# Cross-entropy on one core: rows p and 128+p on partition p, loads divided at the row end, results transposed on VectorE and stored in 128-byte pieces

## The chip, the core and the metric

One core of a Trainium2 chip. The metric is the device time of one execution in microseconds (us), as a median over runs. ScalarE is ACT, VectorE DVE, GpSimd POOL and SyncE SP in the profile; "SPq" is SP's sequencer, which issues the loads of logits and the stores here.

## The reference

For 256 rows of 32,000 float32 logits and one label per row, the kernel returns `log(sum(exp(x))) - x[label]`:

```python
def reference(logits, labels):
    log_probs = logits - np.max(logits, axis=-1, keepdims=True)
    log_probs = log_probs - np.log(np.sum(np.exp(log_probs), axis=-1, keepdims=True))
    return np.array([-log_probs[i, labels[i]] for i in range(batch)]).astype(np.float32)
```

The 32.77 MB of logits have to be read once; 1 KB goes out.

## The kernel before

Partition p holds rows 2p and 2p+1 one after the other, 64,000 columns, which arrive in 14 loads of falling size. ScalarE takes exp of each chunk with a running sum. The logit of the label is gathered, `eg = exp(-g)`, and the result is `Ln(sum * eg)`.

```python
CHUNKS = [14848, 12288, 8832, 6528, 4992, 3776, 2752,
          2368, 1856, 1344, 1344, 1152, 1024, 896]
flat = logits.rearrange("(p r) c -> p (r c)", r=ROWS)
# ... tiles; load(i) issues one chunk, exps(i) sums its exp (two sums where a chunk crosses the row end)
with tc.manual_schedule():
    for i in range(HEAD):
        load(i)
    # ... labels (one 16-byte piece per partition), idx, two indirect gathers into g
    exps(0)
    # ... exps(1), the later loads
    nc.scalar.activation(out=eg[:, :], in_=g[:, :], func=AF.Exp, scale=-1.0)
    # ... exps(2) to exps(12); Ln of the first row on the way
    nc.vector.reduce_sum(out=sums[:, 1:2], in_=parts[1][:, :], axis=mybir.AxisListType.X)
    nc.vector.tensor_mul(out=bias[:, :], in0=sums[:, 1:2], in1=eg[:, 1:2])
    exps(len(CHUNKS) - 1)
    nc.scalar.activation(
        out=res[:, 1:2], in_=s_last[:, :], func=AF.Ln, scale=eg[:, 1:2], bias=bias[:, :]
    )
    nc.sync.dma_start(out=out.rearrange("(p r) -> p r", r=ROWS), in_=res[:, :])
```

The last line stores 128 pieces of 8 bytes, one from each partition, which fill 1 KB of HBM.

The softmax here doesn't subtract the row's maximum and nothing guards it: scores larger than these inputs give would overflow.

Of the kernel before, what the change touches and what calls it, by code (L numbers as in the profile page):

```python
# [2 lines left out]

# [4 lines left out]

P = 128
ROWS = 2  # L10
F32 = mybir.dt.float32
I32 = mybir.dt.int32
AF = mybir.ActivationFunctionType

CHUNKS = [
    14848, 12288, 8832, 6528, 4992, 3776, 2752,
    2368, 1856, 1344, 1344, 1152, 1024, 896,
]
HEAD = 5


@with_exitstack
def kernel(
    ctx: ExitStack,
    tc: tile.TileContext,
    logits: bass.AP,
    labels: bass.AP,
    out: bass.AP,
):
    nc = tc.nc  # L30
    B, C = logits.shape
    assert B == P * ROWS and sum(CHUNKS) == ROWS * C


    flat = logits.rearrange("(p r) c -> p (r c)", r=ROWS)


    pieces = []
    starts = []
    at = 0  # L40
    for n in CHUNKS:
        starts.append(at)
        cuts = [at] + [c for c in range(C, ROWS * C, C) if at < c < at + n] + [at + n]
        pieces.append([(a, b, a // C) for a, b in zip(cuts, cuts[1:])])
        at += n

    head = ctx.enter_context(tc.tile_pool(name="head", bufs=1))
    small = ctx.enter_context(tc.tile_pool(name="small", bufs=1))

    tiles = []  # L50
    for i in range(HEAD):
        tiles.append((head.tile([P, CHUNKS[i]], F32, name=f"x{i}", tag=f"slot{i}"), starts[i]))
    mid = head.tile([P, CHUNKS[1]], F32, name="x_mid", tag="slot1")
    tail = head.tile([P, CHUNKS[0]], F32, name="x_tail", tag="slot0")
    tiles.append((mid, starts[HEAD]))
    for i in range(HEAD + 1, len(CHUNKS)):
        tiles.append((tail, starts[HEAD + 1]))

    n_of = [sum(1 for ps in pieces[:-1] for q in ps if q[2] == r) for r in range(ROWS)]
    parts = [small.tile([P, n_of[r]], F32, name=f"parts{r}") for r in range(ROWS)]  # L60
    s_last = small.tile([P, 1], F32, name="s_last")
    res = small.tile([P, ROWS], F32, name="res")
    sums = small.tile([P, ROWS], F32, name="sums")
    bias = small.tile([P, 1], F32, name="bias")
    lbl = small.tile([P, 2 * ROWS], I32, name="lbl")
    idx = small.tile([P, ROWS], I32, name="idx")
    g = small.tile([P, ROWS], F32, name="g")
    eg = small.tile([P, ROWS], F32, name="eg")

    nc.scalar.preload_act_table_set("natural_log_exp_and_others")  # L70

    lbl_words = dataclasses.replace(
        labels.tensor, shape=[labels.tensor.shape[0] * 2], dtype=I32
    )

    def load(i):
        t, base = tiles[i]
        a, b = starts[i], starts[i] + CHUNKS[i]
        nc.sync.dma_start(out=t[:, a - base:b - base], in_=flat[:, a:b])  # L79

    seen = [0] * ROWS

    def exps(i):
        t, base = tiles[i]
        for a, b, r in pieces[i]:
            if i == len(CHUNKS) - 1:
                acc = s_last[:, :]
            else:
                acc = parts[r][:, seen[r]:seen[r] + 1]
                seen[r] += 1  # L90
            nc.scalar.activation(  # L91
                out=t[:, a - base:b - base],
                in_=t[:, a - base:b - base],
                func=AF.Exp,
                accum_out=acc,
            )

    with tc.manual_schedule():
        for i in range(HEAD):
            load(i)  # L100

        nc.scalar.dma_start(
            out=lbl[:, :], in_=bass.AP(tensor=lbl_words, offset=0, ap=[[2 * ROWS, P], [1, 2 * ROWS]])
        )
        nc.gpsimd.iota(out=idx[:, :], pattern=[[C, ROWS]], base=0, channel_multiplier=ROWS * C)  # L105
        nc.gpsimd.tensor_add(out=idx[:, :], in0=idx[:, :], in1=lbl[:, 0:2 * ROWS:2])  # L106
        for r in range(ROWS):
            nc.gpsimd.indirect_dma_start(  # L108
                out=g[:, r:r + 1],
                out_offset=None,  # L110
                in_=logits[:, :],
                in_offset=bass.IndirectOffsetOnAxis(ap=idx[:, r:r + 1], axis=1),
            )

        exps(0)
        for i in range(HEAD + 1, len(CHUNKS)):
            if i == HEAD + 1:
                exps(1)
                load(HEAD)
            load(i)  # L120
        nc.scalar.activation(out=eg[:, :], in_=g[:, :], func=AF.Exp, scale=-1.0)  # L121
        for i in range(2, len(CHUNKS) - 1):
            exps(i)
            if seen[0] == n_of[0] and i == HEAD - 1:
                nc.vector.reduce_sum(out=sums[:, 0:1], in_=parts[0][:, :], axis=mybir.AxisListType.X)  # L125
                nc.scalar.activation(  # L126
                    out=res[:, 0:1], in_=sums[:, 0:1], func=AF.Ln, scale=eg[:, 0:1]
                )
        nc.vector.reduce_sum(out=sums[:, 1:2], in_=parts[1][:, :], axis=mybir.AxisListType.X)  # L129
        nc.vector.tensor_mul(out=bias[:, :], in0=sums[:, 1:2], in1=eg[:, 1:2])  # L130
        exps(len(CHUNKS) - 1)
        nc.scalar.activation(  # L132
            out=res[:, 1:2], in_=s_last[:, :], func=AF.Ln, scale=eg[:, 1:2], bias=bias[:, :]
        )
        nc.sync.dma_start(out=out.rearrange("(p r) -> p r", r=ROWS), in_=res[:, :])


# [1 line left out]
_INS = ['logits', 'labels']  # L139
_OUTS = [((256,), 'float32')]  # L140


# [23 lines left out]
```

## Time and profile before

| | before |
|---|---|
| median time | 87.25 us (4 runs, 87.14 to 87.51) |
| span of the profiled run | 85.5 us |
| last load landed (last exp starts) | 80.2 us |
| result's store issued | 81.72 us |
| its landing | 84.6 us |

The stream's pace over its whole length stands in a window from 4.5 to 80.2 us (columns: stretch, length, busy time and instructions of DVE, ACT and POOL, clock, DMA share, GB/s):

```profile
4.50:80.20 75.70, 0.16 (x1) 56.24 (x30) 2.26 (x3) 1.00 0.99 420
```

The DMA engines have a share of 0.99: they bound everything up to 80.2. What comes after is the tail. Its last wait is in the waits of the DMA queue (who waited, for what, us in total, times, longest):

```profile
SPq L161 <- DMA out_dram<-res: 2.2, 1, 2.2
```

The end of the program waits 2.2 us for 1 KB to be received.

### The profile page before, as it was taken

The numbers are of one execution on the slowest core, as the hardware profiler recorded it, in microseconds if no ns is written. First come the engines' busy times: TensorE is split into PE (matmuls) and PEld (weight loads), VectorE is DVE, ScalarE is ACT, GpSimd is POOL, SyncE is SP. The second block draws the span as 40 slices with busy tenths as digits, with TensorE's granted clock in tenths as the row PEclk, the third lists the DMA queues.
The fourth block names the chain that finished last, engine by engine and source line by source line (L and its number), as shares of the span: only waits on it lengthen the run. The fifth ranks groups of instructions, "written<-read, shape, count | busy, mean of one in ns | idle before, by whom it ended". The sixth has DMA issues, their size and how long they took to land.

```text
span 85.5 us, 110 instructions
## 1 busy us (share of the span) xinstructions
DVE 0.5 (1%) x3; ACT 59.0 (69%) x34; POOL 2.6 (3%) x8
## 2 busy tenths in 40 slices
DVE  0000000000000000000000000000000000000100
ACT  6000000000999998199999999999999998999920
POOL 1000000000640000000000000000000000000000
DMA  9299999998899998979989998999999999999000
GB/s 361 83 445 445 445 445 445 445 445 368 368 529 506 391 414 368 463 331 496 446 380 428 440 452 375 439 439 392 445 404 427 424 407 415 415 407 389 18 1 0
DMA packets 2368, 32.77 MB, mean 383 GB/s; under 512 B 576, under 2 KB 576, under 8 KB 1344
## 3 DMA queue, kind: packets, MB, share of 16 engines
q1 hardware_dynamic: 2160, 32.77, 90.8%
q10 hardware_dynamic: 144, 0.00, 0.1%
q0 software_dynamic: 64, 0.00, 0.1%
HBM read 32.77 MB, written 0.00 MB: 383 GB/s over the span
## 4 chain that ended last, share of the span: by engine, by line
DMA 73%; issue 13%; ACT 6%; SPq 3%
DMA x<-in_logits_dram 41%; DMA x_tail<-in_logits_dram 32%; ACT x_tail L91 5%; SPq L79 3%; ACT res L132 0%; ACT x L91 0%; ACT eg L121 0%
## 5 line engine op out<-in xcount | busy, mean ns | idle before, releaser
L91 ACT ACTIVATE x<-x 128x14848 f32<-128x14848 f32 (+5 forms) x6 | 40.7, 6790 | 21.5 <-DMA x<-in_logits_dram 21.5
L91 ACT ACTIVATE x_tail<-x_tail 128x1344 f32<-128x1344 f32 (+6 forms) x8 | 12.2, 1525 | 0.5 <-DMA x_tail<-in_logits_dram 0.4
L91 ACT ACTIVATE x_mid<-x_mid 128x3776 f32<-128x3776 f32 x1 | 3.3, 3332 | 0.0
L108 POOL DMA_INDIRECT g<-in_logits_dram,idx x2 | 2.1, 1032 | 0.9 <-POOL idx L106 0.6
L70 ACT ACT_TABLE_LOAD x1 | 1.3, 1283 | 0.7 <-PEq L150 0.7
L91 ACT ACTIVATION_READ_ACCUMULATOR x_tail<-x_tail 128x1 f32 x8 | 1.5, 186 | 0.0
L91 ACT ACTIVATION_READ_ACCUMULATOR x<-x 128x1 f32 x6 | 1.1, 186 | 0.0
L106 POOL TENSOR_TENSOR idx<-idx,lbl 128x2 int32<-128x2 int32 x1 | 0.2, 193 | 20.6 <-DMA lbl<-in_labels_dram 20.6
L125 DVE TENSOR_REDUCE sums<-parts 128x1 f32<-128x3 f32 x1 | 0.2, 156 | 50.9 <-ACT x L91 50.9
L132 ACT ACTIVATE res<-s_last,bias,eg 128x1 f32<-128x1 f32 x1 | 0.4, 387 | 0.0
L129 DVE TENSOR_REDUCE sums<-parts 128x1 f32<-128x11 f32 x1 | 0.2, 165 | 29.3 <-ACT x_tail L91 29.3
L126 ACT ACTIVATE res<-sums,eg 128x1 f32<-128x1 f32 x1 | 0.3, 279 | 0.0
L121 ACT ACTIVATE eg<-g 128x2 f32<-128x2 f32 x1 | 0.2, 187 | 0.0
L91 ACT ACTIVATION_READ_ACCUMULATOR x_mid<-x_mid 128x1 f32 x1 | 0.2, 185 | 0.0
L130 DVE TENSOR_TENSOR bias<-sums,eg 128x1 f32<-128x1 f32 x1 | 0.2, 159 | 0.0
L105 POOL IOTA idx<- 128x2 int32 x1 | 0.1, 120 | 0.4 <-PEq L161 0.4
L150 POOL MEMSET const-uint8-127<- 128x1 uint8 x1 | 0.1, 118 | 0.0
L150 POOL MEMSET const-bfloat16-1.0<- 128x1 bf16 x1 | 0.1, 113 | 0.0
L150 POOL MEMSET const-float32-0.0<- 128x1 f32 x1 | 0.1, 98 | 0.2 <-issue 0.2
L150 POOL MEMSET const-float32-1.0<- 128x1 f32 x1 | 0.1, 104 | 0.0
## 6 DMA issues: line engine op xcount, KB each, us to landing
x<-in_logits_dram SPq DMA_DIRECT2D x1, 7424.0 KB, 20.5
x<-in_logits_dram SPq DMA_DIRECT2D x1, 6144.0 KB, 34.8
x<-in_logits_dram SPq DMA_DIRECT2D x1, 4416.0 KB, 44.8
x<-in_logits_dram SPq DMA_DIRECT2D x1, 3264.0 KB, 52.1
x<-in_logits_dram SPq DMA_DIRECT2D x1, 2496.0 KB, 57.0
x_mid<-in_logits_dram SPq DMA_DIRECT2D x1, 1888.0 KB, 18.1
x_tail<-in_logits_dram SPq DMA_DIRECT2D x1, 1376.0 KB, 21.0
x_tail<-in_logits_dram SPq DMA_DIRECT2D x2, 672.0 KB, 27.0
```

The lines of the kernel that those rows point to most:

```text
L70: nc.scalar.preload_act_table_set("natural_log_exp_and_others")
L79: nc.sync.dma_start(out=t[:, a - base:b - base], in_=flat[:, a:b])
L91: nc.scalar.activation(out=t[:, a - base:b - base], in_=t[:, a - base:b - base], func=AF.Exp, accum_out=acc,)
L106: nc.gpsimd.tensor_add(out=idx[:, :], in0=idx[:, :], in1=lbl[:, 0:2 * ROWS:2])
L108: nc.gpsimd.indirect_dma_start(out=g[:, r:r + 1], out_offset=None, in_=logits[:, :], in_offset=bass.IndirectOffsetOnAxis(ap=idx[:, r:r + 1 ...
L121: nc.scalar.activation(out=eg[:, :], in_=g[:, :], func=AF.Exp, scale=-1.0)
L125: nc.vector.reduce_sum(out=sums[:, 0:1], in_=parts[0][:, :], axis=mybir.AxisListType.X)
L126: nc.scalar.activation(out=res[:, 0:1], in_=sums[:, 0:1], func=AF.Ln, scale=eg[:, 0:1])
L129: nc.vector.reduce_sum(out=sums[:, 1:2], in_=parts[1][:, :], axis=mybir.AxisListType.X)
L130: nc.vector.tensor_mul(out=bias[:, :], in0=sums[:, 1:2], in1=eg[:, 1:2])
L132: nc.scalar.activation(out=res[:, 1:2], in_=s_last[:, :], func=AF.Ln, scale=eg[:, 1:2], bias=bias[:, :])
L150: nc = _bacc.Bacc("TRN2", target_bir_lowering=False, num_devices=1)
```

## The change

Partition p now holds rows p and 128+p, so that the results of one half are 128 neighbours in the output. A 32x32 transpose brings a column of 128 results onto partitions 0, 32, 64 and 96, 32 results each, and the store has 4 pieces of 128 bytes. No load crosses a row end, so 13 loads and 13 exps do; the first half is stored from mid-run; the last sum goes to PSUM. Cut to its core:

```diff
-CHUNKS = [14848, 12288, 8832, 6528, 4992, 3776, 2752, 2368, 1856, 1344, 1344, 1152, 1024, 896]
+BLK = 32
+CHUNKS = [16000, 11008, 4992, 8576, 6272, 4608, 3392, 2560, 1984, 1536, 1216, 1024, 832]
...
-        nc.sync.dma_start(out=t[:, a - base:b - base], in_=flat[:, a:b])
+        nc.sync.dma_start(out=t[:, a - base:a - base + n],
+                          in_=logits[r * P:(r + 1) * P, a - r * C:a - r * C + n])
...
-    s_last = small.tile([P, 1], F32, name="s_last")
-    res = small.tile([P, ROWS], F32, name="res")
+    s_last = psum.tile([P, 1], F32, name="s_last")
+    res = [small.tile([P, BLK], F32, name=f"res{r}") for r in range(ROWS)]
+    res_t = [small.tile([P, BLK], F32, name=f"res_t{r}") for r in range(ROWS)]
...
+    def store(r):
+        nc.vector.transpose(out=res_t[r][:, :], in_=res[r][:, :])
+        nc.sync.dma_start(out=out[r * P:(r + 1) * P].rearrange("(b i) -> b i", i=BLK),
+                          in_=res_t[r][0:P:BLK, :])
...
-            out=lbl[:, :], in_=bass.AP(tensor=lbl_words, offset=0, ap=[[2 * ROWS, P], [1, 2 * ROWS]])
+            out=lbl[:, :, :], in_=bass.AP(tensor=lbl_words, offset=0, ap=[[2, P], [2 * P, ROWS], [1, 2]]),
...
         exps(0)
-        for i in range(HEAD + 1, len(CHUNKS)):
-            if i == HEAD + 1:
-                exps(1)
-                load(HEAD)
+        exps(1)
+        nc.scalar.activation(out=eg[:, :], in_=g[:, :], func=AF.Exp, scale=-1.0)
+        exps(2)
+        for i in range(HEAD, len(CHUNKS)):
             load(i)
-        nc.scalar.activation(out=eg[:, :], in_=g[:, :], func=AF.Exp, scale=-1.0)
...
-        nc.sync.dma_start(out=out.rearrange("(p r) -> p r", r=ROWS), in_=res[:, :])
+        store(1)
```

More of the change, by code (lines that the diff above doesn't have):

```diff
@@ L13 @@
 AF = mybir.ActivationFunctionType
-CHUNKS = [
-    14848, 12288, 8832, 6528, 4992, 3776, 2752,
-    2368, 1856, 1344, 1344, 1152, 1024, 896,
-]
+BLK = 32
+CHUNKS = [16000, 11008, 4992, 8576, 6272, 4608, 3392, 2560, 1984, 1536, 1216, 1024, 832]
 HEAD = 5
+MID_SLOT = 2
 @with_exitstack
@@ L32 @@
     assert B == P * ROWS and sum(CHUNKS) == ROWS * C
-    flat = logits.rearrange("(p r) c -> p (r c)", r=ROWS)
-    pieces = []
-    starts = []
-    at = 0
-    for n in CHUNKS:
-        starts.append(at)
-        cuts = [at] + [c for c in range(C, ROWS * C, C) if at < c < at + n] + [at + n]
-        pieces.append([(a, b, a // C) for a, b in zip(cuts, cuts[1:])])
-        at += n
+    starts = [sum(CHUNKS[:i]) for i in range(len(CHUNKS))]
+    row_of = [a // C for a in starts]
+    assert all((a + n - 1) // C == r for a, n, r in zip(starts, CHUNKS, row_of))
     head = ctx.enter_context(tc.tile_pool(name="head", bufs=1))
     small = ctx.enter_context(tc.tile_pool(name="small", bufs=1))
+    psum = ctx.enter_context(tc.tile_pool(name="psum", bufs=1, space=bass.MemoryType.PSUM))
     tiles = []
@@ L52 @@
         tiles.append((head.tile([P, CHUNKS[i]], F32, name=f"x{i}", tag=f"slot{i}"), starts[i]))
-    mid = head.tile([P, CHUNKS[1]], F32, name="x_mid", tag="slot1")
+    mid = head.tile([P, CHUNKS[MID_SLOT]], F32, name="x_mid", tag=f"slot{MID_SLOT}")
     tail = head.tile([P, CHUNKS[0]], F32, name="x_tail", tag="slot0")
@@ L57 @@
         tiles.append((tail, starts[HEAD + 1]))
-    n_of = [sum(1 for ps in pieces[:-1] for q in ps if q[2] == r) for r in range(ROWS)]
+    n_of = [sum(1 for q in row_of[:-1] if q == r) for r in range(ROWS)]
     parts = [small.tile([P, n_of[r]], F32, name=f"parts{r}") for r in range(ROWS)]
-    s_last = small.tile([P, 1], F32, name="s_last")
-    res = small.tile([P, ROWS], F32, name="res")
+    s_last = psum.tile([P, 1], F32, name="s_last")
+    res = [small.tile([P, BLK], F32, name=f"res{r}") for r in range(ROWS)]
+    res_t = [small.tile([P, BLK], F32, name=f"res_t{r}") for r in range(ROWS)]
     sums = small.tile([P, ROWS], F32, name="sums")
     bias = small.tile([P, 1], F32, name="bias")
-    lbl = small.tile([P, 2 * ROWS], I32, name="lbl")
+    lbl = small.tile([P, ROWS, 2], I32, name="lbl")
     idx = small.tile([P, ROWS], I32, name="idx")
@@ L77, in load @@
         t, base = tiles[i]
-        a, b = starts[i], starts[i] + CHUNKS[i]
-        nc.sync.dma_start(out=t[:, a - base:b - base], in_=flat[:, a:b])
+        a, n, r = starts[i], CHUNKS[i], row_of[i]
+        nc.sync.dma_start(
+            out=t[:, a - base:a - base + n],
+            in_=logits[r * P:(r + 1) * P, a - r * C:a - r * C + n],
+        )
     seen = [0] * ROWS
@@ L84, in exps @@
         t, base = tiles[i]
-        for a, b, r in pieces[i]:
-            if i == len(CHUNKS) - 1:
-                acc = s_last[:, :]
-            else:
-                acc = parts[r][:, seen[r]:seen[r] + 1]
-                seen[r] += 1
-            nc.scalar.activation(
-                out=t[:, a - base:b - base],
-                in_=t[:, a - base:b - base],
-                func=AF.Exp,
-                accum_out=acc,
-            )
+        a, n, r = starts[i] - base, CHUNKS[i], row_of[i]
+        if i == len(CHUNKS) - 1:
+            acc = s_last[:, :]
+        else:
+            acc = parts[r][:, seen[r]:seen[r] + 1]
+            seen[r] += 1
+        nc.scalar.activation(
+            out=t[:, a:a + n], in_=t[:, a:a + n], func=AF.Exp, accum_out=acc
+        )
+    def store(r):
+        nc.vector.transpose(out=res_t[r][:, :], in_=res[r][:, :])
+        nc.sync.dma_start(
+            out=out[r * P:(r + 1) * P].rearrange("(b i) -> b i", i=BLK),
+            in_=res_t[r][0:P:BLK, :],
+        )
     with tc.manual_schedule():
@@ L102 @@
         nc.scalar.dma_start(
-            out=lbl[:, :], in_=bass.AP(tensor=lbl_words, offset=0, ap=[[2 * ROWS, P], [1, 2 * ROWS]])
-        )
-        nc.gpsimd.iota(out=idx[:, :], pattern=[[C, ROWS]], base=0, channel_multiplier=ROWS * C)
-        nc.gpsimd.tensor_add(out=idx[:, :], in0=idx[:, :], in1=lbl[:, 0:2 * ROWS:2])
+            out=lbl[:, :, :],
+            in_=bass.AP(tensor=lbl_words, offset=0, ap=[[2, P], [2 * P, ROWS], [1, 2]]),
+        )
+        for r in range(ROWS):
+            nc.gpsimd.iota(
+                out=idx[:, r:r + 1], pattern=[[1, 1]], base=r * P * C, channel_multiplier=C
+            )
+        nc.gpsimd.tensor_add(out=idx[:, :], in0=idx[:, :], in1=lbl[:, :, 0])
         for r in range(ROWS):
@@ L113 @@
             )
+        for r in range(ROWS):
+            nc.vector.memset(res[r][:, :], 0.0)
         exps(0)
-        for i in range(HEAD + 1, len(CHUNKS)):
-            if i == HEAD + 1:
-                exps(1)
-                load(HEAD)
+        exps(1)
+        nc.scalar.activation(out=eg[:, :], in_=g[:, :], func=AF.Exp, scale=-1.0)
+        exps(2)
+        for i in range(HEAD, len(CHUNKS)):
             load(i)
-        nc.scalar.activation(out=eg[:, :], in_=g[:, :], func=AF.Exp, scale=-1.0)
-        for i in range(2, len(CHUNKS) - 1):
+        for i in range(3, len(CHUNKS) - 1):
             exps(i)
-            if seen[0] == n_of[0] and i == HEAD - 1:
+            if i == HEAD - 1:
                 nc.vector.reduce_sum(out=sums[:, 0:1], in_=parts[0][:, :], axis=mybir.AxisListType.X)
                 nc.scalar.activation(
-                    out=res[:, 0:1], in_=sums[:, 0:1], func=AF.Ln, scale=eg[:, 0:1]
+                    out=res[0][:, 0:1], in_=sums[:, 0:1], func=AF.Ln, scale=eg[:, 0:1]
                 )
+                store(0)
         nc.vector.reduce_sum(out=sums[:, 1:2], in_=parts[1][:, :], axis=mybir.AxisListType.X)
@@ L132 @@
         nc.scalar.activation(
-            out=res[:, 1:2], in_=s_last[:, :], func=AF.Ln, scale=eg[:, 1:2], bias=bias[:, :]
+            out=res[1][:, 0:1], in_=s_last[:, :], func=AF.Ln, scale=eg[:, 1:2], bias=bias[:, :]
         )
-        nc.sync.dma_start(out=out.rearrange("(p r) -> p r", r=ROWS), in_=res[:, :])
+        store(1)
 _INS = ['logits', 'labels']
```

## The prediction

> **What bounds the kernel now.** I read the page first for the busy shares and the chain, then windows over the whole run for the DMA rate, then the issues with their times to landing, and last the timeline of the end. The page:
>
> ```profile
> span 85.5 us, 110 instructions
> DVE 0.5 (1%) x3; ACT 59.0 (69%) x34; POOL 2.6 (3%) x8
> q1 hardware_dynamic: 2160, 32.77, 90.8%
> DMA 73%; issue 13%; ACT 6%; SPq 3%
> ```
>
> The 32.77 MB of logits occupy the sixteen DMA engines for 90.8% of the span, and the chain is 73% DMA. ScalarE (ACT) needs 59.0 us in all, but only what it does after the last landing adds to the end. The windows (columns: stretch, length, busy time of DVE, ACT and POOL, clock, DMA share, GB/s) show whether the stream has room:
>
> ```profile
> 4.50:20.00 15.50, 0.00 (x0) 0.00 (x0) 0.00 (x0) 1.00 1.00 432
> 21.30:46.40 25.10, 0.00 (x0) 23.08 (x4) 2.26 (x3) 1.00 1.00 429
> 46.40:60.10 13.70, 0.16 (x1) 13.57 (x9) 0.00 (x0) 1.00 0.98 418
> 60.10:80.20 20.10, 0.00 (x0) 19.59 (x19) 0.00 (x0) 1.00 0.95 393
> ```
>
> A share of 1.00 means that all sixteen engines are busy: the stream is at their pace from 4.5 us to about 80, whatever the chunks are. So the kernel is a start (some 4 us), 76 us of stream, and an end. The end, from the timeline and from finer windows:
>
> ```profile
> 80.23 0.95 ACT L91 ACTIVATE x_tail<-x_tail 128x896 f32<-128x896 f32 x1
> 81.08 0.19 ACT L91 ACTIVATION_READ_ACCUMULATOR x_tail<-x_tail 128x1 f32 x1
> 81.30 0.39 ACT L132 ACTIVATE res<-s_last,bias,eg 128x1 f32<-128x1 f32 x1
> 81.72 0.35 SPq L135 DMA_DIRECT2D out_dram<-res  x1
> ```
>
> ```profile
> 81.70:82.50 0.80, 0.00 (x0) 0.00 (x0) 0.00 (x0) 1.00 0.00 0
> 82.50:82.80 0.30, 0.00 (x0) 0.00 (x0) 0.00 (x0) 1.00 0.26 4
> 82.80:83.60 0.80, 0.00 (x0) 0.00 (x0) 0.00 (x0) 1.00 0.00 0
> 83.60:84.60 1.00, 0.00 (x0) 0.00 (x0) 0.00 (x0) 1.00 0.00 0
> ```
>
> ```profile
> x<-in_logits_dram SPq DMA_DIRECT2D x1, 7424.0 KB, 20.5
> x_tail<-in_logits_dram SPq DMA_DIRECT2D x1, 448.0 KB, 15.5
> lbl<-in_labels_dram ACTq DMA_DIRECT2D x1, 2.0 KB, 20.7
> out_dram<-res SPq DMA_DIRECT2D x1, 1.0 KB, 2.9
> ```
>
> The result's store is issued at 81.72. Its packets (128 of 8 bytes) all move between 82.5 and 82.8, yet it counts as landed only 2.9 us after its issue, at 84.6. So about 1.8 us pass after the last byte has moved, with nothing running. A load has no such delay: the last one is issued at 64.7, lands 15.5 later at 80.2, and ACT starts at 80.23. The span ends 0.9 after the store, and the measured time is 87.28 - 85.5 = 1.8 above the span.
>
> **What the Trainium skill says.** (1) "DMA: Bandwidth & Descriptors", Anatomy of one DMA: most of a transfer's fixed cost of some 2 us is the receipt of the write, heaviest where the target is HBM; its Specifications add that pieces under 512 B are written by read-modify-write. The 1.8 us of silence agree with the first; that 8-byte pieces cause a part of it no trace here shows yet. (2) Same page, Queues, rings and completion order: an engine takes turns between queues, packet by packet. The trace agrees: the tiny label load (20.7) lands with the first big load (20.5), whose eight packets per engine it has to alternate with. (3) "Perfetto Trace Analysis", Optimizing Scalar/DVE Operations: Scalar's access overhead is about 93 ns on SBUF and 51 on PSUM. The kernel before uses no PSUM, so no number here. (4) "DMA: Bandwidth & Descriptors", Latency and other measured facts: row pitches at large powers of two cut the rate of HBM copies to as little as half. Pitches here are 256,000 bytes before and 128,000 after, 125 times a power of two both; the 432 GB/s show no loss at the first.
>
> **The change part by part.**
>
> *The stream.* Landings follow a simple law. From load 1 (ACT's wait ends at 35.97) to load 4 (issued 3.1, plus 57.0, so 60.1) 20,352 columns take 24.15 us, or 1.187 ns each. The first load: 21.3 - 14,848 x 1.187 = 3.7 us of start. The last nine loads: 16,512 columns in 20.1 us, 0.5 more than 1.187 gives, about 0.06 per load. Columns are still 64,000 and only one load goes, so the last landing is 3.7 + 76.0 + 0.5 = 80.2 again, perhaps 0.06 less. New landings: 22.7, 35.8, 41.8, 51.9, 59.4, 64.9, 69.0, 72.1, 74.5, 76.4, 77.9, 79.2, 80.2.
>
> *ScalarE.* A chunk takes 0.833 ns a column plus 0.20 from start to start (1,856 columns: 73.11 to 74.86). Running this over the new landings: chunk 0 from 22.7 to 36.2, chunk 1 to 45.6, eg to 45.7, chunk 2 to 50.0; then 1.9 idle until chunk 3 lands; chunk 3 to 59.4, chunk 4 to 64.9, Ln to 65.1, the next to 69.1, 72.2, 74.5, 76.4, 77.9, 79.1, and 80.2. The new list is tuned as the old one was: ACT is free when each tail chunk lands, and the last starts at about 80.2. It is 64 columns shorter: -0.05.
>
> *Refills.* The load into the middle slot can be issued only when chunk 2 is done, at 50, rather than 46.55; the queue still holds work until 59.4, so 9 us are to spare. The eight landing semaphores in rotation tie the last load to load 4 (59.4), earlier than before (64.7). Nothing on the path.
>
> *Labels and gather.* The label load becomes two pieces of 8 bytes per partition, 16 instead of 8 packets per engine. Taking turns, eight pass beside load 0 and eight beside load 1, so it lands at about 36 instead of 21.5. Index and first gather take 0.9 and the second issue 1.4 more (21.5 to 22.38 to 23.80 before). Each gather waited for some four big packets (8.1 and 10.4 us beside 49 KB packets of 1.8 us); beside load 2 packets are 20 KB and 0.75 us, so about 3 to 5 us: g at about 42 to 43.5. eg is due at 45.6, and ACT has 1.9 idle after that. I expect no cost.
>
> *The end.* Accumulator and Ln input in PSUM: about 0.04 each, -0.08 (estimate from the page named third). The transpose is one DVE instruction of 32 columns on the path: reductions of 3 and 11 columns take 156 and 165 ns, 1.1 ns a column, so about 0.19, plus one more hand-over of 0.04: +0.23. The issue then comes at 81.72 - 0.05 - 0.08 + 0.23 = 81.8. The store is 4 pieces of 128 bytes on four engines instead of 128 of 8. The 0.8 to its first packet stays; of the 1.8 after it I guess 1.0 remains: -0.75. The other half of the results is stored from mid-run, behind the last loads in the same queue, moves at about 80 and is received by 82, before the last store. Memsets and the first transpose lie beside the stream.
>
> Sum: -0.05 - 0.08 + 0.23 - 0.75 = -0.65, or 86.7. As I am not sure of the receipt, I weigh it down to **86.8 us**.
>
> **The rivals.** (a) *The receipt is a round trip that doesn't depend on the pieces.* For it: the page gives some 2 us for any transfer, and the packets themselves moved within 0.3 us, so their number isn't the visible cost. Against it: 2.9 is above that 2. Then the transpose is a pure cost of 0.1 net: 87.4. Chance about 3 in 10. (b) *The gather comes late.* If the label took longer than its sixteen turns and landed with load 2 (41.8), the gather would go beside 34 KB packets of 1.3 us and g would land near 51; ACT, which holds 38 of its 59 us after that point, would end some 4 us late: 91. Against it stands the turn-taking seen before. 1 in 25. (c) *HBM answers the new order of rows differently*, since a load now comes out of one half of the tensor at half the pitch. The stream is at the engines' pace, not HBM's, which speaks against a gain; a loss of 2% of it would be 1.5 us. 1 in 30. (d) *The chunk list leaves ACT behind in the tail.* My margins are some 0.1 us per chunk, so it could cost 0.2.
>
> **Range and chances.** Main case 86.4 to 87.0, rival (a) 87.3 to 87.5, an untold 0.2 either way, and the runs of before spread 0.4: 86.1 to 87.6. Faster by over 2% needs 85.57, that is 1.75 us; even a store whose receipt vanished would give only 1.7: 0.03. Slower by over 2% needs (b) or (c): 0.04. Within 2%: 0.93.
>
> **What would show it.** Windows at 4.5 to 20 near 432 GB/s and a last chunk that starts at 80.1 to 80.3 show the stream unchanged; the label's landing near 36 and no ACT idle time before eg show the gather free; a transpose under 0.25 us between Ln and an issue near 81.8, and a store of about 2.1 instead of 2.9 us to landing, show the end. The prediction is wrong if the store still takes 2.9 (then 87.4), if eg waits for g, or if the rate differs by over 1%.

## The result, and the profile after

| | before | after |
|---|---|---|
| median time, us | 87.25 (4 runs) | 86.03 (4 runs, 85.94 to 86.19) |
| span, us | 85.5 | 84.4 |
| last exp starts, us | 80.23 | 80.38 |
| last store issued, us | 81.72 | 81.97 |

The ratio is 0.9858, with a 95% interval of 0.983 to 0.9886. A ratio is always the mean time of one kernel's fast runs over that of the other's of the same rounds, so not quite the ratio of the medians. The change is within 2%, on its fast side, and 0.07 us below the range that was predicted.

The page of the changed kernel, first its busy shares and the chain that ended last:

```profile
span 84.4 us, 113 instructions
DVE 1.0 (1%) x7; ACT 58.3 (69%) x30; POOL 2.6 (3%) x9
DMA 59%; ACT 35%; SPq 1%; issue 1%; DVE 0%
```

The chain looks different (ACT 35% instead of 6%), but the receipts show why: in the tail ScalarE starts each chunk within 0.02 to 0.10 us of its landing and is never idle between them, so the walk back follows it instead of the loads. The stream has hardly moved: the last load lands at 80.29 (before: 80.20). Windows:

```profile
46.40:60.10 13.70, 0.16 (x1) 12.49 (x6) 0.00 (x0) 1.00 0.98 420
60.10:80.20 20.10, 0.21 (x1) 20.10 (x16) 0.00 (x0) 1.00 0.95 394
```

```profile
4.50:80.20 75.70, 0.37 (x2) 55.58 (x25) 2.24 (x3) 1.00 0.98 419
```

Before, these stretches moved 418, 393 and 420 GB/s. (Packets count wholly where they start, so short windows near the 64 KB packets of the first load are not compared.) The end, from the timeline:

```profile
80.38 0.88 ACT L87 ACTIVATE x_tail<-x_tail 128x832 f32<-128x832 f32 x1
...
81.17 0.15 ACT L87 ACTIVATION_READ_ACCUMULATOR x_tail<-x_tail 128x1 f32 x1
81.35 0.35 ACT L139 ACTIVATE res<-s_last,bias,eg 128x1 f32<-128x1 f32 x1
81.73 0.21 DVE L93 STREAM_TRANSPOSE res_t<-res 128x32 f32<-128x32 f32 x1 [0.87 <-ACT res L139]
81.97 0.51 SPq L94 DMA_DIRECT2D out_dram<-res_t  x1
```

and from the waits of the DMA queue:

```profile
SPq L168 <- DMA out_dram<-res_t: 0.7, 1, 0.7
```

The store is issued 0.25 later than before, yet the end waits 0.7 us for it instead of 2.2. The trace's semaphore records tell when each DMA engine that takes part has its write received (us; 16 engines before, 4 after):

```
before, issued 81.72: 82.97 83.03 83.04 83.04 83.12 83.19 83.19 83.49 83.64 83.68 83.80 83.87 83.89 84.27 84.35 84.60
after,  issued 81.97: 83.46 83.46 83.48 83.52
```

(After has a fifth record, at 82.90. It is earlier than the first packet, at 83.12, so it is no receipt.) This is the most telling view. Before, the first engine was received 1.25 us after issue, and only the others trailed in, up to 2.88. So up to 1.6 us of the 2.9 was a wait that the first engine did not have, not a fixed round trip. After, all four come within 0.06 us of each other, 1.55 after issue. From the last packet to the last receipt it was 1.8 us before and is 0.3 after.

### The profile page after: what moved, and what is told of

The parts are those of the page before. It is cut to its first block, busy times and chain, and to the rows that moved or that the text cites. A ratio compares the mean times of both kernels' runs of the same rounds, so it can differ in the third digit from the quotient of the medians.

```text
span 84.4 us, 113 instructions
## 1 busy us (share of the span) xinstructions
DVE 1.0 (1%) x7; ACT 58.3 (69%) x30; POOL 2.6 (3%) x9
## 4 chain that ended last, share of the span: by engine, by line
DMA 59%; ACT 35%; SPq 1%; issue 1%; DVE 0%
DMA x<-in_logits_dram 59%; ACT x L87 15%; ACT x_tail L87 14%; ACT x_mid L87 5%; SPq L72 1%; ACT res L139 0%; DVE res_t L93 0%
## 5 line engine op out<-in xcount | busy, mean ns | idle before, releaser
L87 ACT ACTIVATE x<-x 128x16000 f32<-128x16000 f32 (+4 forms) x5 | 40.0, 8004 | 21.2 <-DMA x<-in_logits_dram 21.2
L87 ACT ACTIVATE x_tail<-x_tail 128x3392 f32<-128x3392 f32 (+6 forms) x7 | 11.8, 1690 | 0.0
L87 ACT ACTIVATE x_mid<-x_mid 128x4608 f32<-128x4608 f32 x1 | 4.0, 4026 | 0.0
```

Of the source, the lines that this page charges most:

```text
L87: nc.scalar.activation(out=t[:, a:a + n], in_=t[:, a:a + n], func=AF.Exp, accum_out=acc)
```

## The experiments

My theory after the result: the gain is the store alone, because 8-byte pieces written side by side hold each other up. The rivals: a part comes from the row order and the chunk list; or small pieces are slow in themselves; or the number of pieces or engines counts.

### Stores alone (m1_stores_alone)

Twelve kinds of small store, one at a time, no loads. Each is followed by a memset of its source, which must wait for the receipt:

```diff
+    for (name, words, pat, ap), t in zip(cases, scr):      # scr: internal tensors in HBM
+        nc.sync.dma_start(out=bass.AP(tensor=t, offset=0, ap=pat), in_=ap)
+        nc.vector.memset(src[:, :], 1.0)
```

> A measurement of the disputed cost by itself (wrong result on purpose, no loads): twelve kinds of small store from SBUF to HBM, one after the other with nothing else running, each twice, each followed by a VectorE memset of its source that has to wait for the store to be received. In the kernel before, the 128 pieces of 8 bytes had all moved 1.0 us after issue, and the 16 engines' receipts then came in one by one from 1.25 to 2.88 us after issue; in the changed kernel 4 pieces of 128 bytes were received 1.55 after issue. Theory A (pieces that share a short stretch of HBM wait for each other): 128 of 8 bytes side by side takes about 2.9 us from issue, the same pieces 512 bytes apart take about 1.6, and so does 16 of 8 bytes within 20%. Theory B (every piece that small is slow in itself, wherever it goes): all rows of 8-byte pieces take near 2.9, at any pitch, and only larger pieces (64 bytes and up) come down to 1.6. Theory C (it is the number of pieces or of engines, not their size): 128 pieces of 64 or 512 bytes take 2.9 too, and 16 pieces of 8 bytes take less than 2.

The timeline on DVE (in brackets the idle time before the memset, which is the issue of the store and its receipt; names say pieces and bytes; the two lines of the first name are its two turns):

```profile
5.52 0.17 DVE L53 MEMSET src<- 128x128 f32 x1 [4.52 <-DMA s128of8B<-src]
7.48 0.17 DVE L53 MEMSET src<- 128x128 f32 x1 [1.79 <-DMA s4of128B<-src]
9.22 0.17 DVE L53 MEMSET src<- 128x128 f32 x1 [1.58 <-DMA s128of8B_pitch64B<-src]
...
22.95 0.17 DVE L53 MEMSET src<- 128x128 f32 x1 [7.10 <-DMA s128of4B<-src]
24.94 0.17 DVE L53 MEMSET src<- 128x128 f32 x1 [1.83 <-DMA s16of8B<-src]
...
28.65 0.17 DVE L53 MEMSET src<- 128x128 f32 x1 [1.57 <-DMA s128of32B<-src]
...
32.24 0.17 DVE L53 MEMSET src<- 128x128 f32 x1 [1.69 <-DMA s128of512B<-src]
...
35.26 0.17 DVE L53 MEMSET src<- 128x128 f32 x1 [2.85 <-DMA s128of8B<-src]
```

The same 128 pieces of 8 bytes from the same partitions take 4.52 and 2.85 us side by side, and 1.58 when they are written 64 bytes apart. 128 pieces of 32 or 512 bytes take 1.57 and 1.69. And 64 pieces of 8 bytes side by side out of 4 partitions, with receipts from only four engines, took 2.68 and 3.15. So neither the size in itself (theory B) nor the number of pieces or engines (C) makes the delay: crowding does (A), that is, small pieces that lie side by side. Pieces of 4 bytes are the worst, 7.10 and 7.01. (The 4.52 was the first store of the program. In m2 below, whose list begins with the same store, the two turns took 4.48 and 3.06; why the first is slower is not shown.)

### The store part alone on the old layout (k1_before_with_piece_store)

```diff
+                nc.vector.transpose(out=res_t[:, :, 0], in_=res[0][:, :])    # mid-run, after the first Ln
...
-        nc.sync.dma_start(out=out.rearrange("(p r) -> p r", r=ROWS), in_=res[:, :])
+        nc.vector.transpose(out=res_t[:, :, 1], in_=res[1][:, :])
+        nc.sync.dma_start(out=out.rearrange("(b i r) -> b i r", i=32, r=ROWS), in_=res_t[0:P:32, :, :])
```

> The kernel before, its row order, 14 loads and labels untouched, with the store part of the change alone: two transposes into a tile whose columns interleave the two results, then one store of 4 pieces of 256 bytes. If the store is the whole gain, this gets it: end = last landing 80.2 as before, issue at 81.72 + 0.25 = 82.0, receipt 1.5 later at 83.5 instead of 84.6, so 87.25 - 1.1 = 86.1 us, level with the changed kernel (86.03). If the row order or the chunk list carried a part of the gain, it stays above 86.4.

Measured: 86.16 us (86.13 to 86.37), ratio 0.9873, interval 0.9846 to 0.9899. This is what the store theory expected. Its trace shows the store and the last wait at the end:

```profile
82.05 0.63 SPq L141 DMA_DIRECT2D out_dram<-res_t  x1
```

```profile
SPq L169 <- DMA out_dram<-res_t: 0.7, 1, 0.7
```

The four receipts come 1.58 to 1.64 us after issue. Rows 2p and 2p+1 can stay together on a partition, if the transposes interleave the two results; the new row order isn't needed for the gain.

### The store part undone on the new layout (k2_after_without_transpose)

```diff
-        nc.vector.transpose(out=res_t[r][:, :], in_=res[r][:, :])
-        nc.sync.dma_start(out=out[r * P:(r + 1) * P].rearrange("(b i) -> b i", i=BLK), in_=res_t[r][0:P:BLK, :])
+        nc.sync.dma_start(out=out[r * P:(r + 1) * P].rearrange("(p o) -> p o", o=1), in_=res[r][:, 0:1])
```

> The changed kernel with its store part undone: both results stored straight from their column as 128 pieces of 4 bytes each, no transposes; row order, 13 loads and PSUM kept. If the store is the whole gain: issue at about 81.7, receipt some 2.9 later at 84.6 or a little more, so about 87.2 to 87.3 us, level with the kernel before. If the row order and chunk list carry a part, it falls to 86.7 or below.

Measured: 91.36 us, ratio 1.0487 (1.0441 to 1.0533). My expectation missed by 4 us, because I had taken 4-byte pieces to behave as 8-byte ones. The last store in the list of DMA issues (KB, us to landing):

```profile
out_dram<-res SPq DMA_DIRECT2D x1, 0.5 KB, 7.1
```

It is issued at 81.41 and takes 7.1 us to its last receipt; in the stores alone it was 6.9 and 6.8 (7.10 and 7.01 until the memset). Against the changed kernel that is 0.56 earlier to the issue and 7.1 - 1.55 = 5.6 more after it, or 5.0 in sum; the medians differ by 5.3. (The first half's store, also in 4-byte pieces, was still being received until 84.60, beside the last one. By the stores alone that explains at most 0.3 of the 7.1.) Without the transpose the changed layout is a loss of 4 us against the kernel before: it leaves one result of 4 bytes per partition in place of two, and the transpose makes that harmless.

### The wait for the gather (k3_after_eg_later)

In the changed kernel ScalarE waits 1.4 us for g (forming eg), which was not predicted, and after that only 0.47 for chunk 3:

```profile
47.13 0.20 ACT L124 ACTIVATE eg<-g 128x2 f32<-128x2 f32 x1 [1.38 <-DMA g<-in_logits_dram,idx]
...
52.15 7.35 ACT L87 ACTIVATE x<-x 128x8576 f32<-128x8576 f32 x1 [0.47 <-DMA x<-in_logits_dram]
```

```diff
-        nc.scalar.activation(out=eg[:, :], in_=g[:, :], func=AF.Exp, scale=-1.0)
         exps(2)
+        nc.scalar.activation(out=eg[:, :], in_=g[:, :], func=AF.Exp, scale=-1.0)
```

> The changed kernel with one instruction moved: eg is formed after chunk 2 instead of before it, so ScalarE no longer waits 1.4 us for the late gather. My reading is that the wait cost nothing, because ScalarE waits for chunk 3 at 52.1 in any case: chunk 2 should end at about 50.1 instead of 51.6, chunk 3 start at 52.1 as before, and the time stay at 86.0 within 0.15. The rival is that lateness is handed on down the tail: then up to 0.5 us less.

Measured: 86.26 us (85.96 to 86.47), ratio 0.9884 (0.9846 to 0.9922). No gain. The wait is gone, and the idle time has moved in front of chunk 3, which starts at the same time:

```profile
49.82 0.19 ACT L125 ACTIVATE eg<-g 128x2 f32<-128x2 f32 x1
...
52.14 7.35 ACT L87 ACTIVATE x<-x 128x8576 f32<-128x8576 f32 x1 [2.14 <-DMA x<-in_logits_dram]
```

### What crowding is (m2_stores_crowding)

> Again the store by itself (wrong result on purpose). The first set showed 128 pieces of 8 bytes received 4.3 and 2.7 us after issue side by side, but 1.4 at a pitch of 64 or 512 bytes; 128 of 32 bytes side by side 1.4; 128 of 4 bytes side by side 6.9; 16 of 8 bytes 1.65. So the delay belongs to small pieces that crowd, not to small pieces. What crowding means is open. If sharing a stretch of 64 bytes is what counts, pitches of 16 and 32 bytes (4 and 2 pieces in 64) lie between 1.4 and 2.7, and 16-byte pieces side by side too. If only pieces under 32 bytes that share 32 bytes suffer, a pitch of 32 gives 1.4 and a pitch of 16 does not. If it is pieces of one DMA engine that wait for each other[...], the two spread orders, in which consecutive partitions write 128 or 32 bytes apart though the same stretch is filled in the end, come down to about 1.4; if any piece in the same 64 bytes counts, they stay at about 2.7 and 6.9. 64 and 32 pieces of 8 bytes: half and a quarter of the excess if it is a queue of pieces. And 4 of 128 bytes from neighbouring partitions: first packet 0.82 after issue if the 1.15 seen came from the step of 32 partitions, 1.15 again if it came from having few rows.

The edit is another list of cases, run forward and then backward. Timeline on DVE, five of them, three with both turns:

```profile
16.76 0.17 DVE L51 MEMSET src<- 128x128 f32 x1 [3.70 <-DMA s64of8B<-src]
20.09 0.17 DVE L51 MEMSET src<- 128x128 f32 x1 [3.17 <-DMA s32of8B<-src]
21.71 0.17 DVE L51 MEMSET src<- 128x128 f32 x1 [1.45 <-DMA s16of8B_rows_together<-src]
23.15 0.17 DVE L51 MEMSET src<- 128x128 f32 x1 [1.28 <-DMA s4of128B_rows_together<-src]
...
28.21 0.17 DVE L51 MEMSET src<- 128x128 f32 x1 [3.24 <-DMA s128of8B_spread<-src]
...
45.88 0.17 DVE L51 MEMSET src<- 128x128 f32 x1 [3.21 <-DMA s128of8B_spread<-src]
...
49.00 0.17 DVE L51 MEMSET src<- 128x128 f32 x1 [1.29 <-DMA s4of128B_rows_together<-src]
...
54.08 0.17 DVE L51 MEMSET src<- 128x128 f32 x1 [3.31 <-DMA s32of8B<-src]
```

Three things follow. Neighbouring pieces need not come from neighbouring partitions: in the "spread" store consecutive partitions write 128 bytes apart, and it still takes 3.2 (4-byte pieces likewise 6.8 and 7.2, where consecutive partitions write 64 bytes apart, not 32 as the expectation says). Whether the pieces that collide belong to one DMA engine or to several is not shown, as the packet records name no engine. It isn't a queue in which each piece takes its turn: 32 pieces take as long as 128 do when they are not the program's first store (3.17 and 3.31 against 2.85 and 3.06). And sharing 64 bytes costs only at times: at a pitch of 32 bytes the two turns took 2.02 and 1.62, at 16 bytes 1.56 and 2.66, with 16-byte pieces side by side 1.57 and 1.61. Of the receipts of the 32 pieces, nine come between 1.16 and 1.27 us after issue, and the rest in steps, at 1.69, 2.12, 2.55 and 2.98, so 0.42 to 0.43 apart (in the other turn 1.67, 2.08, 2.69 and 3.12, with one step of 0.6). What exactly collides, and why 16 pieces of 8 bytes escape it, stays open.

The run also shows something useful: 4 pieces of 128 bytes from partitions 0 to 3 take 1.28 and 1.29, against 1.79 and 1.72 from partitions 32 apart, where the store's packets start later after the issue (1.15 to 1.2 instead of 0.7 us). So do 16 pieces from partitions 8 apart (1.16 against 0.80 from neighbours). But 64 pieces from 64 neighbouring partitions start late too (1.16 and 1.12), so the step is not the only thing that delays the start; what else does is open.

### Two attempts at a better version, and the changed kernel again

The first brings the last half onto partitions 0 to 3 with a matmul before Ln:

```diff
...
+        nc.vector.scalar_tensor_tensor(out=total[:, :], in0=quad_eg[:, :], scalar=s_last[:, :],
+                                       in1=quad_bias[:, :], op0=AluOpType.mult, op1=AluOpType.add)
+        nc.tensor.matmul(rows[:, :], lhsT=total[:, :], rhs=place[:, :], start=True, stop=True)
+        nc.scalar.activation(out=fin[:, :], in_=rows[:, :], func=AF.Ln)
+        nc.sync.dma_start(out=out[P:2 * P].rearrange("(b i) -> b i", i=BLK), in_=fin[:, :])
```

> A version meant to beat both kernels. In the second set of stores alone, 4 pieces of 128 bytes were received 1.10 us after issue from neighbouring partitions, but 1.55 in the first set from partitions 32 apart. So the last half is brought onto partitions 0 to 3 by one small matmul with a 0/1 matrix, before the logarithm, which then runs on 4 x 32 elements. Path: sum read, VectorE multiply-add 0.2, matmul with its hand-overs 0.3 to 0.4 (no number in these traces yet), Ln 0.25, against Ln 0.36 and transpose 0.25 in the changed kernel: 0.15 to 0.25 longer to the issue, 0.45 less from issue to receipt. Expected 85.8 us, 0.2 under the changed kernel; if the matmul takes over 0.6, no gain.

The second does it with four transposes into one row:

```diff
...
+            for b in range(P // BLK):
+                rows = slice(b * BLK, (b + 1) * BLK)
+                nc.vector.transpose(out=row[:, rows], in_=res[1][rows, :])
+            nc.sync.dma_start(out=out[P:2 * P].rearrange("(o i) -> o i", o=1), in_=row[0:1, :])
```

> The same aim in another way: four transposes of 32 x 32 in place of one of 128 x 32, all into partitions 0 to 31, so that partition 0 holds the 128 results of the last half as one row of 512 bytes. Each small transpose should take 0.1 to 0.15 us against 0.21 for the one; the issue comes 0.2 to 0.4 later, the receipt 0.45 sooner after it if one row behaves like four neighbouring ones. Expected 85.9 to 86.1 us, level with the changed kernel or 0.1 under it.

> The changed kernel itself, for a comparison in the same rounds: 86.0 us, 0.986 of the kernel before. Also a check on the reading of the first profile: the last store again received 1.5 us after issue, its four engines' receipts within 0.1 us of each other, and ScalarE again waiting 1 to 1.5 us for g before eg without a later start of chunk 3.

| same rounds | median, us | ratio to before | 95% interval |
|---|---|---|---|
| matmul (k4) | 86.15 | 0.9874 | 0.9844 to 0.9904 |
| four transposes (k5) | 86.41 | 0.9907 | 0.9888 to 0.9926 |
| changed kernel again (k6) | 86.26 | 0.9903 | 0.988 to 0.9927 |

Neither is told apart from the changed kernel, and both missed what was expected (85.8, and 85.9 to 86.1) by some 0.3. The timeline of k4 and then that of k5 show why not much was to be had:

```profile
80.71 0.88 ACT L94 ACTIVATE x_tail<-x_tail 128x832 f32<-128x832 f32 x1
...
82.51 0.31 SPq L162 DMA_DIRECT2D out_dram<-fin  x1
```

```profile
81.76 0.84 DVE L96 STREAM_TRANSPOSE row<-res 32x32 f32<-32x32 f32 x4 [0.87 <-ACT res L147]
```

In k4 the last receipt comes at 83.69, so 2.98 after the last exp's start; in k6 it is 83.47 - 80.33 = 3.14. The end became 0.16 shorter, as hoped, but in the profiled run the stream itself was 0.38 later, and such shifts of a few tenths are as large as the gain. In k5 a 32x32 transpose takes 0.21 us, as long as the 128x32 one, where 0.1 to 0.15 was expected, which eats what the store saves (its receipt comes 1.11 after issue). k6 repeats the other readings: receipts at 1.47 to 1.55 us after issue, and eg waiting for g. Its ratio, 0.9903, is a little above that of the first session, so the change is worth some 0.9 to 1.2 us.

## Why the prediction was right or wrong, point by point

- **The bound and the stream: right.** The windows read 419 GB/s against 420 from 4.5 to 80.2, and the last exp started at 80.38 where 80.2 was worked out. The window named as a sign, 4.5 to 20, read 458 instead of 432, but with a DMA share of 1.06, which cannot be: there whole packets are counted where they start. The row pitch of 128,000 bytes cost nothing visible (rival c). That the stream is "at the engines' pace, not HBM's" is not shown by a share of busy engines. Rival (d) cost at most 0.06: the last exp starts 0.09 after its landing, 0.03 before.
- **The step that failed is a term of the sum: "of the 1.8 after it I guess 1.0 remains: -0.75", and the weighing down after it.** The mechanism was right, the size was not. From issue to receipt the store took 1.55 us, not 2.1: 0.3 instead of 1.0 remained after the last packet, and "the 0.8 to its first packet stays" was wrong the other way, 1.15. The semaphore records of before, which I had not read, would have given the size: the first engine was received 1.25 us after issue, so at most 1.6 of the 2.9 were waiting. From the first packet to the last receipt 2.04 us became 0.40, so 1.6 vanished, and 0.3 of it went into the later start (m2: the step of 32 partitions). "A load has no such delay" was a wrong reading too: it compared a landing with ScalarE's start, not with the last packet. The last load's packets ended at 79.77 and its receipt came at 80.20, 0.43 later: a hint that far less than 1.0 could remain.
- **Rival (a), that the receipt doesn't depend on the pieces: refuted** by k1 and by the stores alone. I had given it 3 in 10 and moved the forecast 0.1 up for it. The page's 2 us is a fit for DMAs that GpSimd issues, not "for any transfer", and the 1.8 us of silence, which I took to agree with it, was mostly crowding.
- **The rest of the end: right.** Read and Ln with PSUM took 0.15 and 0.35 instead of 0.19 and 0.39 (0.08 expected; read from the durations, not run by itself), transpose and hand-over 0.24 (0.23), the shorter chunk 0.07 (0.05). The issue came at 81.97 for 81.8, since the last exp started 0.15 late.
- **Label: right. Gather: wrong, at no cost.** The label landed at 35.85 ("about 36"). But g was there at 47.0, not at 42 to 43.5: the gathers took 7.7 and 8.9 us from issue to landing, hardly less than the 8.1 and 10.4 of before, though the packets beside them took 0.74 to 1.3 us instead of 1.8. The step "beside load 2 packets are 20 KB and 0.75 us, so about 3 to 5 us" scaled all of it, but the packet records show a part that stayed the same: 3.8 us pass from the end of the first gather's instruction to its first packet, and 3.7 before. By the prediction's own sign ("if eg waits for g") this step failed. "I expect no cost" held, through the slack in front of chunk 3 (k3), of which 0.47 of the 1.9 us was left: the margin saved it, not the estimate.
- **Range:** with the store's two errors put right the sum would have been 86.7 - 0.55 = 86.15, against 86.03 and, in the second session, 86.26. (The 86.7 starts from 87.32, the median of the three runs known then; from 87.25 it is 86.05.) The main case went down to 86.4 only, since the receipt was taken as 2.1 us at the best guess.

## What to carry to other kernels

Look at the last store of a kernel by its receipts, engine by engine, before calling its latency fixed: here the spread among them was a wait that could be taken away. Where each partition has 4 or 8 bytes to write into one short stretch of HBM, gather them first into larger pieces (32 bytes and more showed no delay here); a transpose of 0.21 us took 1.3 us off the time from issue to receipt. A changed layout can need such a repair, so price the store it leads to (7.1 us for 128 pieces of 4 bytes) together with it.

## What the Trainium skill lacked or had wrong

- "DMA: Bandwidth & Descriptors", Specifications, gives 512 B as the least size for full rate, with read-modify-write below. No run here tests the rate, or shows whether the delay is that read-modify-write. Small size alone cost nothing in latency here: 128 pieces of 8 bytes at a pitch of 64 bytes took 1.58 us, of 32 bytes side by side 1.57, of 512 bytes 1.69. What costs is 4- or 8-byte pieces side by side (7.1 and 2.8 to 4.5 us). No page has this, nor that 16 pieces of 8 bytes side by side escape it (1.45 and 1.83).
- The same page, Anatomy of one DMA (there for GpSimd's path), puts most of a fixed 2 us into the receipt of the write. For the uncrowded stores from SyncE to HBM, nothing else running, 1.28 to 1.84 us passed from before the issue to the reader of the semaphore, of which 0.3 to 0.4 from the last packet to the last receipt. So neither the 2 us nor its division carries over to these stores.
- No page has it that a store whose source steps over partitions starts later: first packet 1.2 us after issue from partitions 32 apart, 0.7 from neighbours, 4 pieces of 128 bytes both (1.79 and 1.28 us in all).
- "VectorE: DVE Perf Modes", The three transpose paths, gives one time for a 128x128 bf16 transpose (311 ns); in fp32 the runs show 211 ns for 128x32 and about the same for 32x32 (0.84 us for four).
- "Perfetto Trace Analysis", Optimizing Scalar/DVE Operations, gives 93 and 51 ns for Scalar, so 42 between SBUF and PSUM, as busy times, and says that profiled latency is about twice that. The profiled durations here fell by some 40 ns each, not by 84 (the read of the sum from 0.19 to 0.15 us, Ln from 0.39 to 0.35): as a difference, the busy figure fits.
